# The sample state update as whole tiles on GpSimd, and a causal mask taken with a Relu, in an SSD mixer

## The chip, the core and the metric

The kernel runs on one core of one Trainium2 chip. The core has TensorE (PE, with its weight loads listed apart as PEld), VectorE (DVE), ScalarE (ACT), GpSimd (POOL) and SyncE (SP, which here only issues transfers). Each engine takes its instructions strictly in the order of its own queue and waits on semaphores for the others. The metric is the device time of one execution in microseconds (us).

## The reference, cut to what matters

One inference step of a trunk of two layers serves a prompt of 512 tokens and 8 samples of one token each. Layer 0 mixes tokens with sparse attention, layer 1 with a Mamba-2 state space mixer (SSD); each is followed by a squared-ReLU MLP. The change lies in the SSD mixer:

```python
a_cum = jnp.cumsum(chunk(dt * a), axis=2)
causal = np.tril(np.ones((L, L), dtype=bool))[:, :, None, None]
seg = a_cum[:, :, :, None] - a_cum[:, :, None, :]
decay = jnp.exp(jnp.where(causal, seg, NEG))
cb = jnp.einsum('bclgn,bcsgn->bclsg', cc, bc)
y_diag = jnp.einsum('bclsg,bclsgr,bcsgrp->bclgrp', cb, decay, xdt)
...
def step(state, inp):
    cs, cd = inp
    return state * cd[..., None, None] + cs, state
...
y_off = jnp.einsum('bclgn,bcgrpn,bclgr->bclgrp', cc, prev, jnp.exp(a_cum))
```

For the prompt there are 32 heads in 4 groups; a_cum is a cumulative sum of negative numbers along the tokens. For a sample the scan has one step: new state = old state * exp(dt a) + dt x B, and y = C . new state; the state of all samples is 8 x 32 x 64 x 128 numbers (8 MB), read from memory and written back.

## The kernel before, in words

Activations lie with the features on the 128 partitions and 520 columns (512 prompt tokens, 8 samples). Every large product is made of units of 24 or 48 matmuls with fp32r operands: weights are split into a high part (ScalarE copy, L330, tile `wh`) and a low part (VectorE subtraction, L336, tile `wh`), two products ahead of their use, and three terms are accumulated.

The mixer (`ssd`, L1643) walks a list `SSD_SEQ` over 16 pairs of heads, q = 0..15, four to a group. For each group `ssd_bc` makes B and C with a convolution each, B.C (`cb`, one 128x512 tile), the transposed B (`bt`) and the samples' B and C on all partitions (`bc`, 128 x 2 x 8 x 128). For each pair there are four steps:

- `x`: `ssd_x` makes the product and its convolution (`conv`, L1435: three VectorE multiply-adds of 128x512, a Tanh, one more VectorE operation, and small ones for the samples).
- `pair`: `ssd_pair` (L1503). Two matmuls spread a_cum of a head over the partitions, two more add the causal mask (`negsR`, 0 or -1e30); eight Exp on ScalarE with a bias give `M`, and VectorE multiplies it by `cb`. Another matmul (`sp`) and an Exp give `E` for the off-chunk term. Then come transposes of X, `xd`, the chunk states `st`, the outputs `yd` and `yo`, and `y`. At its end stands the sample update: for each of 8 samples ScalarE makes B times dt x (`xb`), VectorE the new state (L1462, tile `ss`) and, with a third operand and an accumulator, the sample's y. The state is loaded by SP (`ssd_state`) and stored by the GpSimd queue.
- `z`: `ssd_gate` makes the gate's product and multiplies y with it. The sum of squares `yss` is added up on GpSimd (L1602), one 128x520 addition for a pair.
- `out`: after the first pair of the next group, the output product of the group before (`ssd_out`, 8 units of 24 matmuls, added up by VectorE).

The `x` step of pair q+1 stands before the `pair` step of q in the list (after the next group's `bc` at the end of a group). The order in an engine's queue is not the order of the source alone: a scheduler, when the program is built, places instructions by their readiness in its own model of times, and by source order among the ready ones; so rows of neighbouring steps are interleaved. Tiles come from pools with a fixed number of buffers: `ss` 2, `xb` 3, `s` (PSUM) 4, `a` (PSUM, the large products) 2, `M` 2, `cv` 2, `z` 1.

Of the kernel before, what the change touches and what calls it, by code (L numbers as in the profile page):

```python
# [22 lines left out]
NEG = -1e30  # L23
# [3 lines left out]
CONST_COLS = [('ident', 128), ('tri', 128), ('e2', 32), ('negq', 128), ('negs', 128), ('selb', 256),  # L27
# [9 lines left out]
def shape_constants():  # L37
    c = np.zeros((128, NCONST), np.float32)

    def put(name, a):  # L40
        o, w = CONST_AT[name]
        c[:a.shape[0], o:o + w] = a

    i = np.arange(128)
    put('ident', np.eye(128, dtype=np.float32))
    put('negq', np.where(i[None, :] <= i[:, None], 0.0, NEG))
    put('tri', (i[:, None] <= i[None, :]).astype(np.float32))
    put('negs', np.where(i[:, None] <= i[None, :], 0.0, NEG))
    t = np.arange(4)[None, :, None] * 128 + i[:, None, None]
    ok = (16 * np.arange(32)[None, None, :] + 31 <= t) & (np.arange(32) < 31)  # L50
    put('cadd', np.where(ok, 0.0, NEG).reshape(128, 128))
    put('cmul', ok.astype(np.float32).reshape(128, 128))
    j, hc = i // 32, i % 32
    gp, r, e = hc // 8, (hc // 2) % 4, hc % 2
    live = hc < 16
    g = 2 * gp + e
    b = np.arange(8)
    put('selb', np.stack([(b[:, None] == 4 * k + j[None, :]) & live[None, :] for k in range(2)], 1)
        .astype(np.float32).reshape(8, 256))
    put('gsel', ((np.arange(16)[None, :] == (g * 4 + r)[:, None]) & live[:, None]).astype(np.float32))  # L60
    put('gmask', ((np.arange(4)[None, :] == g[:, None]) & live[:, None]).astype(np.float32))
    put('gsum', ((j[:, None] == j[None, :]) & (g[:, None] == g[None, :]) & live[:, None] & live[None, :]).astype(np.float32))
    put('sel2', (((j[:, None, None] == np.arange(4)[None, None, :]) & (r[:, None, None] == np.arange(4)[None, :, None])
                  & live[:, None, None]).astype(np.float32)).reshape(128, 16))
    put('e2', (i[:, None] % 32 == np.arange(32)[None, :]).astype(np.float32))
    put('jc', np.broadcast_to(np.arange(1, 7, dtype=np.float32), (128, 6)))
    return c
# [163 lines left out]
def ck(c):  # L231
    return slice(c * 128, (c + 1) * 128)
# [29 lines left out]
class Step:  # L262
# [393 lines left out]
    def setup_late(self):  # L656
# [6 lines left out]
        t = self.tile('s', [128, 256])  # L663
        self.aux(t[:, 0:128], I['const'][:, CONST_AT['negq'][0]:CONST_AT['negq'][0] + 128])
        self.aux(t[:, 128:256], I['const'][:, CONST_AT['negs'][0]:CONST_AT['negs'][0] + 128])
        self.negqR = self.const([128, 128], F32R, self.pn)
        self.vcopy(self.negqR, t[:, 0:128])
        self.negsR = self.const([128, 128], F32R)
        self.vcopy(self.negsR, t[:, 128:256])
# [687 lines left out]
    def dt_fin(self, ps):  # L1357
# [50 lines left out]
        self.nac, self.cd, self.dtde = (m[:, ck(n)].rearrange("p (c h) -> p c h", c=4) for n in range(3))  # L1408
        fl = "p c h -> p (c h)"
        self.ts(self.nac.rearrange(fl), p[:, 0:128], -1.0)  # L1410
# [53 lines left out]
    def ssd_bc(self, g, first):  # L1464
# [10 lines left out]
        self.copy(cb, p)  # L1475
# [27 lines left out]
    def ssd_pair(self, g, t, X, G, w):  # L1503

        q = 4 * g + t
        C, cb, bt, xs, bc = (G[k] for k in ('C', 'cb', 'bt', 'xs', 'bc'))
# [3 lines left out]
        for e in range(2):  # L1510
            r = slice(64 * e, 64 * e + 64)
            self.mm(ps[e], self.e2R[r, 2 * q + e:2 * q + e + 1].to_broadcast([64, 128]), self.ac2[r], True, False)
        for e in range(2):
            self.mm(ps[e].rearrange("p (c l) -> p c l", c=4), self.identR,
                    self.negsR[:, None, :].to_broadcast([128, 4, 128]), False, True)
        for e in range(2):
# [3 lines left out]
            for c in range(4):  # L1520
                self.act(m[:, ck(c)], p[:, ck(c)], AF.Exp, bias=self.nac[:, c, h:h + 1])
            self.tt(m, m, cb, ALU.mult)
            M.append(m)
        sp = self.tile('sp', [64, 2, 64], F32R)
        self.nc.gpsimd.tensor_copy(sp, self.e2R[0:64, 2 * q:2 * q + 2, None].to_broadcast([64, 2, 64]))
        p = self.tile('s', [128, 512])
        self.mm(p[:, 128:512], sp.rearrange("p a b -> p (a b)"), self.ac2[0:64, 128:512], True, True)
        E = self.tile('E', [128, 512])
        self.act(E[:, 128:512], p[:, 128:512], AF.Exp)
# [43 lines left out]

        x8 = self.small([128, 8], 'x8', 2)
        self.tt(x8, xs[:, 2 + t], self.sdb[:, q, 0, :], ALU.mult)
        ys = self.small([128, 8], 'ys', 2)
        for b in range(8):
            v = w[:, b]
            x = self.tile('xb', [128, 128])
            self.act(x, bc[0][:, b], AF.Copy, scale=x8[:, b:b + 1])  # L1580
            self.pool_stt(v, v, self.sdb[:, q, 1, b:b + 1], x, ALU.mult, ALU.add)
            self.stt(x, v, 1.0, bc[1][:, b], ALU.mult, ALU.mult, accum_out=ys[:, b:b + 1])
        self.store(self.O['ssm_s'][q], w.rearrange("p b n -> p (b n)"))
# [59 lines left out]
    def ssd(self, h):  # L1643
# [10 lines left out]
        X = {}  # L1654
        for kind, n in SSD_SEQ:
# [3 lines left out]
            elif kind == 'x':  # L1659
                G[g] = G_next  # L1660
                X[n] = self.ssd_x(g, t, G[g])
            elif kind == 'pair':
                y = self.ssd_pair(g, t, X.pop(n), G[g], self.ssd_state(n))
# [217 lines left out]
    def build(self, stop=None):  # L1881
# [17 lines left out]
        with self.tc.tile_pool(name='e', bufs=1) as self.pe:  # L1899
# [6 lines left out]
            with self.phase('s', {'g': 5, 'cv': 2, 'x': 2, 'th': 2, 'xd': 3, 'st': 2, 'M': 2, 'E': 1, 'y': 1, 'z': 1,  # L1906
                                  'acc': 8, 'bc': 1, 'ss': 2, 'xb': 3, 'yss': 1, 'yh': 8, 'sp': 1,
# [62 lines left out]
```

## Time and profile before

| what | value |
|---|---|
| median of the runs | 1722.26 us (3 runs, 1722.0 to 1723.0) |
| the profiled execution, its own time | 1719.56 us |
| its span in the trace | 1717.9 us |
| granted TensorE clock, mean | 0.993 of full speed |
| PE, PEld busy | 1664.7 us (97%), 1538.2 us (90%) |
| DVE, ACT, POOL busy | 984.0, 761.6, 143.5 us (57, 44, 8%) |

Busy time is the union of an engine's instructions. Matmuls are pipelined and their ends are modelled, so a busy PE can still lose time between two starts. A DVE or POOL row that waits for something after it has started counts that as its own duration. Starts are given in us from the span's beginning, and the mixer lies from about 888 to 1335.

### The profile page before, as it was taken

How to read it: one execution, taken by the hardware profiler on the slowest of the kernel's cores; microseconds unless marked ns; L12 is line 12 of the kernel's file. 1: busy time of each engine (PE TensorE's matmuls, PEld its weight loads, DVE VectorE, ACT ScalarE, POOL GpSimd, SP SyncE). 2: the span in 40 equal slices, each digit the busy share in tenths (PEclk: the TensorE clock that was granted, in tenths of full speed). 3: DMA queues.
4: the chain of work that ended last, by engine and by line, in shares of the span. 5: the costliest groups of instructions: out<-in, count | busy, mean ns of one | idle time of the engine just before them, and what ended most of it. 6: DMA issues, size and time to landing. Idle time of an engine off the chain costs nothing.

```text
span 1717.9 us, 34708 instructions
## 1 busy us (share of the span) xinstructions
PE 1664.7 (97%) x13878; PEld 1538.2 (90%) x13878; DVE 984.0 (57%) x2423; ACT 761.6 (44%) x1624; POOL 143.5 (8%) x303
## 2 busy tenths in 40 slices
PE   7899999999999999999999999999998999999997
PEld 6699877667989999999989898899987999999997
DVE  2543377776464343433478968879797643434344
ACT  3534366666443131322456666646564422323231
POOL 2000112310001000000001102111022000000000
PEclk9999999999999999999999999999999999999999
DMA  8822656545433523333433442344324232323321
GB/s 302 288 87 99 215 195 223 169 148 196 137 126 97 184 87 135 99 135 136 136 135 102 135 166 90 117 135 138 125 89 160 74 99 87 96 90 93 93 86 51
DMA packets 72114, 229.87 MB, mean 134 GB/s; under 512 B 8770, under 2 KB 15218, under 8 KB 71186
## 3 DMA queue, kind: packets, MB, share of 16 engines
q1 hardware_dynamic: 62546, 198.45, 35.1%
q0 software_dynamic: 8832, 28.16, 4.5%
q8 instruction: 109, 1.79, 0.4%
q10 hardware_dynamic: 576, 1.05, 0.2%
q14 instruction: 51, 0.42, 0.1%
HBM read 204.02 MB, written 23.61 MB: 133 GB/s over the span
## 4 chain that ended last, share of the span: by engine, by line
PE 71%; DVE 8%; ACT 2%; issue 1%; POOLq 0%; DMA 0%; SPq 0%; POOL 0%; DVEq 0%; ACTq 0%
PE a L323 60%; PE s L323 5%; PE f L323 2%; PE o L323 1%; DVE wh L336 1%; PE sc L323 1%; PE t L327 1%; DVE c L345 1%; DVE g L345 1%; ACT wh L330 1%; DVE acc L336 1%; PE s L327 0%; DVE ss L1462 0%; PE f L327 0%; ACT h L333 0%
## 5 line engine op out<-in xcount | busy, mean ns | idle before, releaser
L323 PE MATMUL a<-h,wh 128*128 128x256 f32 x5952 | 743.4, 284 | 3.8 <-ACT t L333 1.6
L323 PEld LDWEIGHTS a<-h,wh 128*128 128x128 f32 x5952 | 723.3, 189 | 10.1 <-issue 3.7
L330 ACT ACTIVATE wh<-w 128x1024 fp32r<-128x1024 f32 x212 | 224.5, 1059 | 521.8 <-PE a L323 480.4
L336 DVE TENSOR_TENSOR wh<-w,wh 128x1024 fp32r<-128x1024 f32 x212 | 259.6, 1225 | 266.4 <-ACT wh L330 265.8
L323 PEld LDWEIGHTS a<-hid,wh 128*128 128x128 f32 x3072 | 370.2, 188 | 5.0 <-issue 4.2
L323 PE MATMUL a<-hid,wh 128*128 128x256 f32 (+1 forms) x3072 | 373.7, 283 | 0.0
L336 DVE TENSOR_TENSOR t<-a,c 128x8 f32<-128x8 f32 x72 | 12.0, 167 | 217.4 <-PE a L323 217.4
L323 PE MATMUL a<-yh,wh 128*128 128x256 f32 (+1 forms) x768 | 98.4, 285 | 3.0 <-DVE acc L336 1.5
L323 PEld LDWEIGHTS a<-yh,wh 128*128 128x128 f32 x768 | 93.7, 188 | 5.2 <-DVE acc L336 2.2
L330 ACT ACTIVATE hid<-t 128x520 fp32r<-128x520 f32 x64 | 40.9, 639 | 84.5 <-DVE t L336 84.5
L330 ACT ACTIVATE h<-t 128x128 f32<-128x128 f32 (+3 forms) x128 | 52.5, 440 | 46.5 <-PE t L327 46.3
L333 ACT ACTIVATE h<-sc,m 128x128 f32<-128x128 f32 (+3 forms) x128 | 66.6, 530 | 14.6 <-DVE m L340 12.5
L336 DVE TENSOR_TENSOR hid<-t,hid 128x520 fp32r<-128x520 f32 x64 | 44.7, 700 | 42.3 <-ACT hid L330 42.3
L327 PE MATMUL t<-c,h 128*128 128x128 f32 x320 | 53.5, 281 | 1.9 <-DVE h L340 0.7
L345 DVE SCALAR_TENSOR_TENSOR c<-a,c,c 128x512 f32<-128x512 f32 (+1 forms) x74 | 53.9, 728 | 1.8 <-PE a L323 1.8
L333 ACT ACTIVATE xb<-bc,x 128x128 f32<-128x128 f32 x128 | 46.4, 419 | 15.8 <-DVE xb L345 11.2
L323 PE MATMUL sc<-kv,q 128*128 128x128 f32 (+3 forms) x128 | 49.5, 387 | 0.0
L323 PEld LDWEIGHTS a<-q,wh 128*128 128x128 f32 x384 | 46.3, 188 | 1.0 <-ACT wh L330 0.8
L327 PEld LDWEIGHTS t<-c,h 128*128 128x128 f32 x320 | 34.4, 141 | 13.8 <-issue 7.7
L323 PE MATMUL a<-q,wh 128*128 128x256 f32 (+1 forms) x384 | 46.7, 283 | 0.0
L323 PE MATMUL sc<-kv,c 128*128 128x128 f32 (+3 forms) x128 | 42.3, 331 | 4.2 <-POOL c L947 4.2
L1462 DVE SCALAR_TENSOR_TENSOR ss<-ss,c,xb 128x128 f32<-128x128 f32 x128 | 43.3, 361 | 4.4 <-ACT xb L333 4.2
(366 smaller groups left out, 1941.9 us busy)
## 6 DMA issues: line engine op xcount, KB each, us to landing
w<-in_w_dram SPq DMA_DIRECT2D x128, 512.0 KB, 3.5
w<-in_ada_w_dram SPq DMA_DIRECT2D x80, 512.0 KB, 3.6
w<-in_w_ssd_dram SPq DMA_DIRECT2D x40, 512.0 KB, 3.6
w<-in_w_nsa_dram SPq DMA_DIRECT2D x20, 512.0 KB, 3.6
ss<-in_ssm_dram SPq DMA_DIRECT2D x16, 512.0 KB, 4.3
out_ssm_s_dram<-ss POOLq DMA_DIRECT2D x16, 512.0 KB, 3.0
w<-in_w_sout_dram SPq DMA_DIRECT2D x16, 512.0 KB, 4.1
cm<-in_cmp_dram SPq DMA_DIRECT2D x24, 256.0 KB, 4.0
```

Source lines behind the costliest of these rows:

```text
L323: self.nc.tensor.matmul(out, lhsT, rhs, start=start, stop=stop, skip_group_check=True)
L327: self.nc.tensor.transpose(out, in_, self.C('ident')[0:k, 0:k])
L330: self.nc.scalar.activation(out, in_, AF.Copy, **kw)
L333: self.nc.scalar.activation(out, in_, f, **kw)
L336: self.nc.vector.tensor_tensor(out, a, b, op=op)
L345: self.nc.vector.scalar_tensor_tensor(out, a, s, b, op0=op0, op1=op1, **kw)
L1462: self.nc.vector.scalar_tensor_tensor(out, a, s, b, op0=op0, op1=op1)
```

## The change

The causal mask leaves the PSUM accumulation: `cb` is multiplied once a group by the 0/1 triangle `tri` (VectorE, in place of a ScalarE copy), the two mask matmuls of a pair go, and so that the exponential can't overflow above the diagonal, eight ScalarE Relu with scale -1 make max(0, a_s - a_l), over which two Exp of 128x512 with scale -1 are taken. `E` is read from the same two PSUM tiles (two Exp of 64x384), so that the `sp` copy on GpSimd and its matmul go. The constant `negs` and its loading go.

The sample update becomes a function of its own, called right after the `x` step, that is one pair earlier. It holds four GpSimd tensor-tensor operations over a whole 128 x 8 x 128 tile (state by its decay, B by dt x, their sum, the sum by C), and one VectorE reduction to the 8 numbers of y. The eight ScalarE and sixteen VectorE operations (with eight accumulator reads) of a pair go. `xb` becomes one buffer of 128 x 1024.

```diff
@@ ssd_bc
-        self.copy(cb, p)
+        self.tt(cb.rearrange("p (c l) -> p c l", c=4), p.rearrange("p (c l) -> p c l", c=4),
+                self.C('tri')[:, None, :].to_broadcast([128, 4, 128]), ALU.mult)
@@ ssd_pair
+    def ssd_sample(self, g, t, G):
         q = 4 * g + t
+        xs, bc = G['xs'], G['bc']
+        v = self.ssd_state(q)
+        x8 = self.small([128, 8], 'x8', 2)
+        self.tt(x8, xs[:, 2 + t], self.sdb[:, q, 0, :], ALU.mult)
+        sh = [128, 8, 128]
+        x = self.tile('xb', sh)
+        f = self.nc.gpsimd.tensor_tensor
+        f(v, v, self.sdb[:, q, 1, :, None].to_broadcast(sh), op=ALU.mult)
+        f(x, bc[0], x8[:, :, None].to_broadcast(sh), op=ALU.mult)
+        f(v, v, x, op=ALU.add)
+        f(x, v, bc[1], op=ALU.mult)
+        ys = self.small([128, 8], 'ys', 3)
+        self.nc.vector.tensor_reduce(ys, x, AX.X, ALU.add)
+        self.store(self.O['ssm_s'][q], v.rearrange("p b n -> p (b n)"))
+        return ys
...
-            self.mm(ps[e], self.e2R[r, 2 * q + e:2 * q + e + 1].to_broadcast([64, 128]), self.ac2[r], True, False)
-        for e in range(2):
-            self.mm(ps[e].rearrange("p (c l) -> p c l", c=4), self.identR,
-                    self.negsR[:, None, :].to_broadcast([128, 4, 128]), False, True)
+            self.mm(ps[e], self.e2R[r, 2 * q + e:2 * q + e + 1].to_broadcast([64, 128]), self.ac2[r], True, True)
...
-                self.act(m[:, ck(c)], p[:, ck(c)], AF.Exp, bias=self.nac[:, c, h:h + 1])
+                self.act(m[:, ck(c)], p[:, ck(c)], AF.Relu, scale=-1.0, bias=self.ac[:, c, h:h + 1])
+
+            self.act(m, m, AF.Exp, scale=-1.0)
             self.tt(m, m, cb, ALU.mult)
             M.append(m)
-        sp = self.tile('sp', [64, 2, 64], F32R)
-        self.nc.gpsimd.tensor_copy(sp, self.e2R[0:64, 2 * q:2 * q + 2, None].to_broadcast([64, 2, 64]))
-        p = self.tile('s', [128, 512])
-        self.mm(p[:, 128:512], sp.rearrange("p a b -> p (a b)"), self.ac2[0:64, 128:512], True, True)
         E = self.tile('E', [128, 512])
-        self.act(E[:, 128:512], p[:, 128:512], AF.Exp)
+        for e in range(2):
+            r = slice(64 * e, 64 * e + 64)
+            self.act(E[r, 128:512], ps[e][r, 128:512], AF.Exp)
...
-        x8 = self.small([128, 8], 'x8', 2)
-        self.tt(x8, xs[:, 2 + t], self.sdb[:, q, 0, :], ALU.mult)
-        ys = self.small([128, 8], 'ys', 2)
-        for b in range(8):
-            v = w[:, b]
-            x = self.tile('xb', [128, 128])
-            self.act(x, bc[0][:, b], AF.Copy, scale=x8[:, b:b + 1])
-            self.pool_stt(v, v, self.sdb[:, q, 1, b:b + 1], x, ALU.mult, ALU.add)
-            self.stt(x, v, 1.0, bc[1][:, b], ALU.mult, ALU.mult, accum_out=ys[:, b:b + 1])
-        self.store(self.O['ssm_s'][q], w.rearrange("p b n -> p (b n)"))
@@ ssd
                 X[n] = self.ssd_x(g, t, G[g])
+                Y[n] = self.ssd_sample(g, t, G[g])
             elif kind == 'pair':
-                y = self.ssd_pair(g, t, X.pop(n), G[g], self.ssd_state(n))
+                y = self.ssd_pair(g, t, X.pop(n), G[g], Y.pop(n))
```

## Rows read from the trace of the kernel before

**Rows 1.** The page: busy us, share of the span, instructions of PE.

```profile
PE 1664.7 (97%) x13878; PEld 1538.2 (90%) x13878; DVE 984.0 (57%) x2423; ACT 761.6 (44%) x1624; POOL 143.5 (8%) x303
```

**Rows 2.** Busy time by stretch: the four stretches that are dense with pairs.

```profile
core 0: us, PE busy (x) PEld busy (x) DVE busy (x) ACT busy (x) POOL busy (x), PEclk, DMA share, GB/s
913.40:1000.70 87.30, 86.78 (x688) 79.06 (x688) 79.94 (x238) 62.48 (x171) 14.36 (x28) 1.00 0.42 142
1038.60:1104.20 65.60, 64.73 (x517) 58.87 (x515) 57.76 (x161) 42.92 (x115) 11.90 (x21) 1.00 0.35 116
1143.40:1209.20 65.80, 65.09 (x531) 60.27 (x529) 59.22 (x164) 42.77 (x107) 11.99 (x22) 1.00 0.37 116
1248.60:1292.00 43.40, 43.15 (x350) 37.78 (x351) 40.04 (x118) 27.09 (x74) 8.77 (x12) 1.00 0.29 88
```

**Rows 3.** The same stretches, tile xb alone: us, DVE busy, ACT busy.

```profile
913.40:1000.70 87.30, 17.11 (x96) 11.24 (x32) 1.00 0.42 142
1038.60:1104.20 65.60, 11.31 (x57) 6.96 (x19) 1.00 0.35 116
1143.40:1209.20 65.80, 12.52 (x57) 6.78 (x19) 1.00 0.37 116
1248.60:1292.00 43.40, 10.98 (x48) 5.94 (x16) 1.00 0.29 88
```

**Rows 4.** PE in time order: start us, us, then line and operation; one pair's start.

```profile
1157.76 1.16 PE L323 MATMUL s<-c,c 64*128 64x512 f32 x4
1158.85 0.43 PE L323 MATMUL s<-c,sp 64*128 64x384 f32 x1
1159.22 0.66 PE L327 MATMUL s<-c,x 128*128 128x128 f32 x4
```

**Rows 5.** DVE groups by form, 1143.4 to 1209.2: busy us, mean ns, idle before.

```profile
L336 DVE TENSOR_TENSOR wh<-w,wh 128x1024 fp32r<-128x1024 f32 x9 | 11.0, 1222 | 3.1 <-ACT wh L330 3.1
...
L345 DVE SCALAR_TENSOR_TENSOR st<-st,c,s 128x64 f32<-128x64 f32 x18 | 4.0, 274 | 0.0
...
L345 DVE SCALAR_TENSOR_TENSOR y<-x,c,s 128x512 f32<-128x512 f32 x3 | 2.2, 742 | 0.0
...
L1462 DVE SCALAR_TENSOR_TENSOR x<-th,x 128x512 f32<-128x512 f32 x3 | 2.1, 693 | 0.7 <-ACT th L333 0.7
...
L336 DVE TENSOR_TENSOR xd<-s,c 128x512 f32<-128x512 f32 x3 | 2.0, 676 | 0.0
```

**Rows 6.** POOL and ACT by tile: duration ns min/median/max, first and last start.

```profile
L1602 POOL TENSOR_TENSOR yss<-yss,z x14: 1289/1311/1572, 950.5 to 1279.8; 128x520 f32<-128x520 f32 x14
...
L1525 POOL CAST sp<-c x16: 281/333/898, 888.5 to 1264.5; 64x128 fp32r<-64x128 f32 x16
...
L333 ACT ACTIVATE M<-s,c x128: 352/380/423, 915.1 to 1277.5; 128x128 f32<-128x128 f32 x128
```

**Rows 7.** POOL's memset of three columns, a group: busy us, mean ns, idle.

```profile
L1439 POOL MEMSET cv<- 128x3 f32 x24 | 2.4, 102 | 77.7 <-DVE xs L340 33.1 <-DVE xs L1454 12.6 <-DVE x L345 12.6
```

**Rows 8.** DVE and POOL in time order around two additions of L1602.

```profile
949.43 0.74 DVE L345 SCALAR_TENSOR_TENSOR x<-cv,c,x 128x512 f32<-128x512 f32 x1
950.47 1.57 POOL L1602 TENSOR_TENSOR yss<-yss,z 128x520 f32<-128x520 f32 x1 [1.54 <-ACT z L333]
950.79 1.80 DVE L345 SCALAR_TENSOR_TENSOR x<-cv,c,x 128x512 f32<-128x512 f32 x1
...
1174.27 0.68 DVE L336 TENSOR_TENSOR xd<-s,c 128x512 f32<-128x512 f32 x1
1174.64 1.30 POOL L1602 TENSOR_TENSOR yss<-yss,z 128x520 f32<-128x520 f32 x1 [3.02 <-ACT z L333]
```

**Rows 9.** Waits of PE, and of SP's queue, in the mixer: us, times, longest.

```profile
PE s L323 <- DVE xd L336: 1.2, 5, 0.3
...
SPq L351 <- DMA out_ssm_s_dram<-ss: 45.5, 12, 11.7
```

**Rows 10.** A table load on ACT within the mixer.

```profile
891.72 1.28 ACT L333 ACT_TABLE_LOAD   x1
```

More of the change, by code (lines that the diff above doesn't have):

```diff
@@ L23 @@
 NEG = -1e30
-CONST_COLS = [('ident', 128), ('tri', 128), ('e2', 32), ('negq', 128), ('negs', 128), ('selb', 256),
+CONST_COLS = [('ident', 128), ('tri', 128), ('e2', 32), ('negq', 128), ('selb', 256),
               ('cadd', 128), ('cmul', 128), ('gsum', 128), ('gsel', 16), ('gmask', 4), ('sel2', 16), ('jc', 6)]
@@ L47, in shape_constants @@
     put('tri', (i[:, None] <= i[None, :]).astype(np.float32))
-    put('negs', np.where(i[:, None] <= i[None, :], 0.0, NEG))
     t = np.arange(4)[None, :, None] * 128 + i[:, None, None]
@@ L662, in setup_late @@
         self.tt(self.wg[1], wg, self.wg[0], ALU.subtract)
-        t = self.tile('s', [128, 256])
+        t = self.tile('s', [128, 128])
         self.aux(t[:, 0:128], I['const'][:, CONST_AT['negq'][0]:CONST_AT['negq'][0] + 128])
-        self.aux(t[:, 128:256], I['const'][:, CONST_AT['negs'][0]:CONST_AT['negs'][0] + 128])
         self.negqR = self.const([128, 128], F32R, self.pn)
         self.vcopy(self.negqR, t[:, 0:128])
-        self.negsR = self.const([128, 128], F32R)
-        self.vcopy(self.negsR, t[:, 128:256])
         u = self.U('np')
@@ L1407, in dt_fin @@
         m = self.m[0].rearrange("p a b -> p (a b)")
-        self.nac, self.cd, self.dtde = (m[:, ck(n)].rearrange("p (c h) -> p c h", c=4) for n in range(3))
+        self.ac, self.cd, self.dtde = (m[:, ck(n)].rearrange("p (c h) -> p c h", c=4) for n in range(3))
         fl = "p c h -> p (c h)"
-        self.ts(self.nac.rearrange(fl), p[:, 0:128], -1.0)
+        self.vcopy(self.ac.rearrange(fl), p[:, 0:128])
         self.copy(ae, p[:, 128:256])
@@ L1501, in ssd_state, with ssd_pair @@
         return w
-    def ssd_pair(self, g, t, X, G, w):
+    def ssd_sample(self, g, t, G):
         q = 4 * g + t
-        C, cb, bt, xs, bc = (G[k] for k in ('C', 'cb', 'bt', 'xs', 'bc'))
+        xs, bc = G['xs'], G['bc']
[13 more added lines that the diff above has]
+        return ys
+    def ssd_pair(self, g, t, X, G, ys):
+        q = 4 * g + t
+        C, cb, bt, xs = (G[k] for k in ('C', 'cb', 'bt', 'xs'))
         M = []
@@ L1653, in ssd @@
         first = [pb]
-        X = {}
+        X, Y = {}, {}
         for kind, n in SSD_SEQ:
@@ L1906, in build @@
             with self.phase('s', {'g': 5, 'cv': 2, 'x': 2, 'th': 2, 'xd': 3, 'st': 2, 'M': 2, 'E': 1, 'y': 1, 'z': 1,
-                                  'acc': 8, 'bc': 1, 'ss': 2, 'xb': 3, 'yss': 1, 'yh': 8, 'sp': 1,
+                                  'acc': 8, 'bc': 1, 'ss': 2, 'xb': 1, 'yss': 1, 'yh': 8,
                                   'sq': 'M', 'x7': 'M', 'ssq': 'st', 'ad': 'xd', 'dt': 'acc'}) as self.ps, \
```

## The prediction, made before the change was run

> **What bounds the kernel now.** I read the engine shares first: TensorE is busy for 97% of the span [rows 1], so outside the mixer nothing that the change touches can matter. Within the mixer I cut the time at the stretches that are dense with pairs, between them lie the output products. There PE is busy 98 to 99%, but DVE is not far behind: 79.94 of 87.30 us, 57.76 of 65.60, 59.22 of 65.80 and 40.04 of 43.40, some 90% [rows 2]. ACT has a third of its time free and POOL most of it. PE waits for DVE hardly ever, 1.2 us in five places for `xd` [rows 9], so today PE sets the pace and DVE keeps up with little to spare. The change takes work from both and gives POOL much; whether DVE still keeps up is what decides.
>
> **PE.** In one pair's start the four matmuls of `ps` take 1.09 us from the first start to the start of the next group, of which the two mask matmuls are half, 0.545; the `sp` matmul takes 0.37 to the transposes' start [rows 4]. A pair saves 0.915 us, sixteen pairs 14.6 us. This is the most that the change can bring while PE sets the pace.
>
> **ACT.** The `xb` work (6.78 of 42.77 us in the third stretch [rows 2, 3]) goes. Eight Relu stand where eight Exp stood, at the same 0.38 us [rows 6]. Two Exp of 128x512 and one more `E` Exp are new. No row shows an Exp of that size; it costs between one and four of the 128x128 rows, 0.38 to 1.52 us, so three new ones cost at most 4.6 us a pair, 14 us in a stretch with three pairs: 42.77 - 6.78 + 14 = 50 of 65.8 us, still free. I count ACT at nothing; its cover is that spare time. That a Relu between the Exp makes ACT load a table is not seen in a row: the bounds are nothing and two loads of 1.28 us a pair [rows 10], and even these fit into the spare time. I take nothing.
>
> **DVE's own work.** The whole `xb` work goes: 17.11, 11.31, 12.52 and 10.98 us of the four stretches [rows 3]. Added is one reduction of 128x1024 for each `x` step (`ssd_sample` follows it). The nearest row is the subtraction over as many columns, 1.22 us [rows 5], of which some 0.08 overlap with the next; I take 1.14, with bounds of 1.0 and 1.3. There are three `x` steps in the third stretch [rows 5]; by the code's list I count 4, 3, 3 and 2. The masked `cb` adds 0.6 in each of the first three (an operation of 128x512 is 0.68 to 0.74 us with its overlap [rows 5]). What is left as DVE's own is 79.94 - 17.11 + 4.56 + 0.6 = 68.0 us, and in the same way 50.5, 50.7 and 31.3.
>
> **POOL's four operations.** The only row of this kind has 520 columns: 1.311 us at the median [rows 6]. In proportion 1024 columns are 2.58; with the 0.10 of a memset of three columns [rows 7] as the fixed part they are 0.10 + 1.21 x 1024/520 = 2.48. From below: POOL's copy with one input takes 0.28 us at best for 128 columns [rows 6], (0.28 - 0.10)/128 = 1.4 ns a column, 1.54 us for 1024, if an operand that repeats one number costs no read. I take 2.48, as all four have two inputs like the row, and keep 1.54 to 2.6 for the range.
>
> [...]
>
> **What POOL does to DVE.** This is the term that turns the sign. While POOL adds `yss`, a DVE operation with two SBUF operands doesn't run: the convolution's multiply-add takes 0.74 us alone and 1.80 us when it starts into the addition, and ends 0.55 us after it; the addition itself, begun at 950.47 beside a running DVE operation, takes 1.57 instead of 1.31 [rows 8]. So each waits for the other, for a whole instruction. An operation with one operand in PSUM is not held: `xd` from 1174.27 and an addition from 1174.64 overlap, and both take their usual 0.68 and 1.30 us [rows 8].
>
> [...]
>
> So in a dense stretch DVE's time is its own work, plus POOL's operations, less what DVE does beside them without the lock. Whether it idles at the reduction or is held by the lock makes no difference. I count POOL's operations: four for each `x` step, of which one in a stretch falls outside, as the decay of the state needs no `x8` and can run early, or as the last comes late: 15, 11, 11 and 8 (the fourth has its two whole), 37.2, 27.3, 27.3 and 19.8 us. What runs beside them: in the third stretch `st`, `y` and `xd`, which read PSUM, make 4.0 + 2.2 + 2.0 = 8.2 us [rows 5], and the reductions 3.4; of these 11.6 I take 8 as covered, and in proportion to the own work 11, 8, 8 and 5 (bounds: none, and all of it with as much again of the kinds that I left out, 16). DVE's time is then
>
> 68.0 + 37.2 - 11 = 94.2 against 87.3: +6.9
> 50.5 + 27.3 - 8 = 69.8 against 65.6: +4.2
> 50.7 + 27.3 - 8 = 70.0 against 65.8: +4.2
> 31.3 + 19.8 - 5 = 46.1 against 43.4: +2.7
>
> Together +18.0 us. This lets DVE idle nowhere else, though in these four stretches it idled 25 us before (262.1 - 236.96 [rows 2]); of that I leave an eighth, +3. Between the stretches, where DVE has few rows, PE keeps its gain for three pairs: -2.7. The sum is +18.3, rounded +19 for the first pair's burst, which I did not count.
>
> **What moves with it.** The state's load is issued on SP one pair earlier, and its store on POOL's queue after the four operations. SP waits 45.5 us in all for such stores today, and PE for none of it [rows 9]; with two `ss` buffers and a burst that ends a pair before its `y` I count nothing. Behind a burst of four (10 us, some 13 with DVE's turns between) stand on POOL the memset and copy of the next convolution, `ssm_p`'s store and `yss`, whose tile `z` has one buffer. The `x` steps follow each other at 22 us on the mean (three in 65.8 us [rows 2, 5]), so this costs nothing while POOL starts at once; a late start is part of rival (c). The reduction waits for POOL at the head of DVE's queue, and behind it stand the next pair's `M` and `xd`, for which PE waits. The setup's one load and copy less lie off the path: nothing.
>
> **The rivals.**
> (a) *PE goes on setting the pace.* If POOL's operations take p us, the four sums give 45 p - 93.6 + 0.3 = 45 p - 93.3 with the 3 us and the -2.7; the sign turns at p = 2.07. At the lower bound of 1.54, or at 2.48 with twice the cover (64 us instead of 32), the sum is at -14 or below, DVE keeps up everywhere in the dense stretches, and the gain is PE's 14.6 us at most: 1708. For it: PE absorbs the 1.3 us holds of today. Against: the row of 1.311 for half the columns. Chance 0.23.
> (b) *A wash*: p near 2.07 to 2.15, or the lead of two products in the weights hides more of DVE's lag: 1719 to 1726. Chance 0.13.
> (c) *The reduction blocks DVE.* If the queue's order, made when the program is built, puts the reduction before POOL can be done, DVE idles through the bursts and the 32 us of cover are lost: +19 + 32, some 1773. For it: a model that ignores the lock. Against: the order of before left PE almost no wait. Chance 0.10.
> The forecast, slower by the lock, has 0.54.
>
> **How the numbers follow.** The sum is made on the profiled execution (1719.56 us, span 1717.9); the median of the runs is 1722.26, 2.7 above, and a difference carries over. 1722.3 + 19 = 1741.3. The forecast's own range is 1727 (p = 2.2) to 1760 (half of the cover lost). For eight in ten I go from 1711, which leaves out the fullest gain of (a), to 1766, which leaves out most of (c). A measurement of this kernel tells some 0.2% (3.4 us) from no change. Faster takes (a) and a little of (b), 0.25; same 0.12; slower takes the forecast and (c), 0.63.
>
> **What the profile afterwards would show.** Right: POOL rows of 128x1024 at 2.4 to 2.6 us, 64 of them; DVE rows with two SBUF operands of 2 us and more beside them; DVE busy in the dense stretches near 100% although its own work has shrunk; PE idle before `xd`, `M` and `wh` rows in the tens of us. The `ps` group of a pair at 0.55 us either way. Wrong: POOL operations under 2 us, or holds that are short, and the mixer shorter by some 14 us. A long idle of DVE before the reduction would show (c).

## The result and the profile after

The changed kernel takes 1787.20 us at the median of its runs (1781.31 to 1791.49), the kernel before 1722.55 beside it: 3.7% slower, ratio 1.0372 with a 95% interval of [1.0351, 1.0393]. The forecast said slower by 19 us; it is 65 by the medians. The profiled execution took 1786.26 us, with a span of 1784.6.

The page of the changed kernel, its busy times (us, share of the span, instructions) and its chain of waits by engine (followed back from the last instruction to what released each step), and below them the chain of the kernel before:

```profile
PE 1690.4 (95%) x13830; PEld 1554.9 (87%) x13830; DVE 973.4 (55%) x2058; ACT 747.8 (42%) x1540; POOL 281.8 (16%) x350
...
PE 60%; DVE 11%; POOL 6%; ACT 2%; issue 2%; DMA 1%; POOLq 0%; SPq 0%; DVEq 0%; ACTq 0%
...
PE 71%; DVE 8%; ACT 2%; issue 1%; POOLq 0%; DMA 0%; SPq 0%; POOL 0%; DVEq 0%; ACTq 0%
```

Against [rows 1] POOL's busy time has doubled and DVE's has shrunk by 11 us. On the chain PE has fallen from 71% to 60%, DVE has risen from 8% to 11%, and POOL, with nothing before, holds 6%.

**Where the 67 us of span lie.** I cut both traces at two POOL instructions that the change doesn't touch: the `acc` memset (L1371, now L1367) with which the mixer begins, and the first `st` addition (L534, now L533) after the last pair. From that addition to the end both kernels take the same, 412.8 us. Between the two marks, "the mixer" from here on, the kernel before takes 416.85 us and the changed one 474.06: +57.2. The other 9.4 lie ahead of the mixer, in attention, which the change leaves alone. There the granted clock of one stretch differs. Stretches of the changed kernel: in its first profile, and below in a second profile of the same code (columns: stretch, us, busy time of each engine with its instructions, granted clock, DMA share, GB/s):

```profile
220.00:240.00 20.00, 20.00 (x111) 13.57 (x111) 6.45 (x25) 9.47 (x27) 0.58 (x2) 0.50 0.03 2
```

```profile
220.00:240.00 20.00, 19.96 (x197) 14.81 (x196) 13.60 (x54) 15.40 (x46) 2.96 (x7) 1.00 0.35 114
```

In the first, PE works through this stretch without a pause at a granted clock of 0.50 and runs 111 matmuls; in the second it stays at 1.00 and runs 197. In the 20 us ahead of it PE was busy for 17.4 us in the first and 16.2 in the second, with a mean granted clock of 0.83 in both; what decides between the two isn't shown here. Four more runs of the changed kernel fell in two groups, 1779.4 and 1780.1 against 1788.4 and 1791.8 us. Profiles of experiments show the low stretch with the old samples' update and with the new one, with the setup edit and without it. So 9 to 10 of the 67 us come or stay away with the single execution, and the change itself costs the 57 us of the mixer. The second profile gives 474.06 us for the mixer again.

**Inside the mixer.** Waits between the two marks of the changed kernel (us in all, times, longest):

```profile
DVE ys L1515 <- POOL xb L1513: 51.8, 16, 6.0
POOL ss L1510 <- DMA ss<-in_ssm_dram: 32.0, 9, 7.9
PE s L322 <- DVE xd L335: 22.4, 10, 7.8
POOL xb L1511 <- DVE x L335: 13.4, 10, 2.9
PE a L322 <- DVE c L347: 10.6, 2, 5.3
PE a L322 <- DVE acc L335: 5.1, 2, 3.1
PE s L322 <- ACT xd L329: 4.2, 3, 2.4
```

The reduction waits for POOL in all sixteen pairs, 51.8 us, and PE's wait for `xd` has gone from 1.2 us [rows 9] to 22.4. POOL waits for DVE's `x8` (dt x, printed as `x<-xs,c`) in turn. One pair shows how the pieces hang together. DVE, PE and POOL of the changed kernel in order of time (start us, us, instruction, idle before it):

```profile
1076.27 0.17 DVE L335 TENSOR_TENSOR x<-xs,c 128x8 f32<-128x8 f32 x1
...
1083.40 1.22 DVE L1515 TENSOR_REDUCE ys<-xb 128x8 f32<-128x1024 f32 x1 [3.84 <-POOL xb L1513]
...
1090.78 1.75 DVE L344 SCALAR_TENSOR_TENSOR y<-xs,c,ys 128x8 f32<-128x8 f32 x1
...
1095.38 0.68 DVE L335 TENSOR_TENSOR M<-M,g 128x512 f32<-128x512 f32 x1
...
1096.83 0.17 DVE L335 TENSOR_TENSOR x<-xs,c 128x8 f32<-128x8 f32 x1
```

```profile
1076.52 1.90 POOL L1511 TENSOR_TENSOR xb<-bc,x 128x1024 f32<-128x1024 f32 x1 [1.90 <-DVE x L335]
1078.50 2.39 POOL L1512 TENSOR_TENSOR ss<-ss,xb 128x1024 f32<-128x1024 f32 x1
1080.97 2.40 POOL L1513 TENSOR_TENSOR xb<-ss,bc 128x1024 f32<-128x1024 f32 x1
...
1090.15 2.35 POOL L1510 TENSOR_TENSOR ss<-ss,c 128x1024 f32<-128x1024 f32 x1
```

```profile
1089.70 1.16 PE L322 MATMUL s<-xd,g 128*128 128x128 f32 x8 [1.04 <-DVE xd L335]
1090.61 4.30 PE L322 MATMUL a<-h,wh 128*128 128x256 f32 x34
1096.99 0.73 PE L322 MATMUL s<-M,xd 128*64 128x128 f32 x4 [2.08 <-DVE x L335]
```

`x8` ends at 1076.44, and three POOL operations follow one after the other, B times x (1.90 us), the sum and the product with C (2.39 and 2.40), to 1083.37. DVE has less than that to do between `x8` and the reduction, so it stands idle for 3.84 us; `xd` comes late and PE waits 1.04 us. In ten of the sixteen pairs B times x begins within 0.1 us of the end of `x8`, and in all sixteen the reduction starts 6.8 to 8.6 us after B times x: this chain of three, with the reduction close behind `x8` in DVE's queue, is the wait. Then POOL's next operation begins at 1090.15, and `y<-xs,c,ys`, eight columns, 0.22 us otherwise, takes 1.75 and ends when POOL does. DVE doesn't idle from there to 1097.00, so all that stands behind it in its queue moves back, `M` at 1095.38 and the next `x8` at 1096.83, which the view names as what PE waited for, and PE idles 2.08 us. What follows is one more cost. The same place of the changed kernel in stretches of 5 us (the last three columns: granted clock, DMA share, GB/s):

```profile
1095.00:1100.00 5.00, 3.00 (x15) 1.76 (x15) 3.20 (x12) 4.57 (x14) 2.94 (x3) 0.74 0.02 3
1100.00:1105.00 5.00, 5.00 (x21) 3.63 (x19) 1.88 (x2) 1.14 (x4) 4.82 (x4) 0.50 0.02 8
1105.00:1110.00 5.00, 5.00 (x31) 4.33 (x30) 4.42 (x9) 3.70 (x9) 0.00 (x0) 0.73 0.65 215
1110.00:1115.00 5.00, 5.00 (x49) 4.50 (x47) 4.96 (x7) 3.98 (x14) 4.22 (x3) 1.00 0.36 107
```

From the idle time on the granted clock is 0.74, 0.50 and 0.73 in three stretches: (0.26 + 0.50 + 0.27) x 5 = 5.2 us of full-speed work lost at this place, more than the idle time itself (1.04 + 2.08). Summed in this way over stretches of 5 us, the changed kernel loses 18.8 us of its mixer to the lower clock, the kernel before nothing. (Some 2.4 of the 18.8 fall into idle time: weighted with PE's busy share in stretches of 1 us they are 16.4.) The 57.2 us are then +43.4 of PE's idle time (4.4 before, 474.06 - 426.30 = 47.8 after), +18.8 of lower clock, and -5.0 of PE's work at full speed, which is what is left over. Not every stop costs clock: in the 5 us from 1162.7 PE is busy for 1.9, and the granted clock stays at 1.00 there and in the 5 us behind.

### The profile page after: what moved, and what is told of

Read it like the earlier page. It is cut to its first block, busy times and chain, and to the rows that moved or that the text cites. A ratio compares the mean times of both kernels' runs of the same rounds, so it can differ in the third digit from the quotient of the medians.

```text
span 1784.6 us, 34130 instructions
## 1 busy us (share of the span) xinstructions
PE 1690.4 (95%) x13830; PEld 1554.9 (87%) x13830; DVE 973.4 (55%) x2058; ACT 747.8 (42%) x1540; POOL 281.8 (16%) x350
## 3 DMA queue, kind: packets, MB, share of 16 engines
q10 hardware_dynamic: 576, 1.05, 0.2%
## 4 chain that ended last, share of the span: by engine, by line
PE 60%; DVE 11%; POOL 6%; ACT 2%; issue 2%; DMA 1%; POOLq 0%; SPq 0%; DVEq 0%; ACTq 0%
PE a L322 52%; PE s L322 2%; POOL ss L1512 2%; POOL xb L1513 2%; DVE wh L335 2%; PE f L322 2%; POOL xb L1511 1%; PE o L322 1%; PE sc L322 1%; DVE x L344 1%; PE t L326 1%; DVE c L344 1%; DVE yh L344 1%; DVE M L335 1%; DVE acc L335 1%
## 5 line engine op out<-in xcount | busy, mean ns | idle before, releaser
L322 PE MATMUL a<-h,wh 128*128 128x256 f32 x5952 | 757.3, 286 | 3.7 <-ACT t L332 1.6
L335 DVE TENSOR_TENSOR wh<-w,wh 128x1024 fp32r<-128x1024 f32 x212 | 267.7, 1263 | 268.7 <-ACT wh L329 266.6
L322 PE MATMUL a<-yh,wh 128*128 128x256 f32 (+1 forms) x768 | 106.3, 295 | 16.8 <-DVE c L347 10.6
L322 PEld LDWEIGHTS a<-yh,wh 128*128 128x128 f32 x768 | 98.7, 196 | 22.4 <-DVE c L347 11.1
L332 ACT ACTIVATE h<-sc,m 128x128 f32<-128x128 f32 (+3 forms) x128 | 66.5, 530 | 14.6 <-DVE m L339 12.5
L1367 POOL MEMSET acc<- 128x160 f32 x1 | 0.2, 237 | 347.6 <-DVE h L335 347.6
L1515 DVE TENSOR_REDUCE ys<-xb 128x8 f32<-128x1024 f32 x16 | 19.5, 1220 | 51.8 <-POOL xb L1513 51.8
L965 DVE TENSOR_REDUCE m<-sc 128x1 f32<-128x384 f32 (+1 forms) x64 | 38.0, 616 | 17.0 <-PE sc L322 16.9
```

The costliest lines, as they stand in the source:

```text
L322: self.nc.tensor.matmul(out, lhsT, rhs, start=start, stop=stop, skip_group_check=True)
L332: self.nc.scalar.activation(out, in_, f, **kw)
L335: self.nc.vector.tensor_tensor(out, a, b, op=op)
L965: self.nc.vector.tensor_reduce(m[:, k:k + 1], ss[k][:, 0:w], AX.X, ALU.max)
L1367: nc.gpsimd.memset(x, 0.0)
L1515: self.nc.vector.tensor_reduce(ys, x, AX.X, ALU.add)
```

## The experiments

All figures of the mixer are between the two marks; PE's idle time is the mixer less PE's busy time there; "clock" is the sum over 5-us stretches of their length times one less the granted clock. "POOL" is the busy time of the whole-tile operations on it, "wait" DVE's at the reduction. The ratios below are against runs of the kernel before beside each experiment, whose medians were 1721.3 to 1729.3 us; the mixer's time doesn't hold the low stretch in attention and is the better measure.

| kernel | mixer us | PE idle | clock | DVE busy | POOL | wait |
|---|---|---|---|---|---|---|
| before | 416.9 | 4.4 | 0.0 | 348.7 | - | - |
| changed | 474.1 | 47.8 | 18.8 | 338.7 | 147.0 | 51.8 |
| mask half alone | 415.2 | 9.6 | 1.7 | 349.8 | - | - |
| samples' half alone | 488.6 | 56.9 | 25.6 | 359.0 | 147.7 | 38.6 |
| reduction without the wait | 446.4 | 31.5 | 8.5 | 356.3 | 146.6 | - |
| no GpSimd operations | 416.3 | 9.4 | 3.4 | 308.0 | - | - |
| reduction at the pair's end | 469.6 | 42.9 | 18.8 | 355.4 | 150.6 | 24.5 |
| eight memsets | 418.9 | 11.2 | 1.7 | 316.5 | 122.9 | 2.7 |
| ten memsets | 426.5 | 14.2 | 8.5 | 321.0 | 153.3 | 4.8 |
| two of four operations | 429.8 | 17.1 | 8.6 | 330.8 | 62.5 | - |
| mask half, B x on GpSimd | 435.4 | 25.7 | 8.6 | 357.5 | 38.3 | - |
| mask half, no copies | 419.9 | 9.7 | 1.7 | 350.5 | - | - |
| mask half, whole tiles on DVE | 433.5 | 20.2 | 13.7 | 375.6 | - | - |

### The two halves

The mask half is the diff ahead of the prediction without `ssd_sample`; the pair keeps the eight steps at its end.

```
-                Y[n] = self.ssd_sample(g, t, G[g])
-                y = self.ssd_pair(g, t, X.pop(n), G[g], Y.pop(n))
+                y = self.ssd_pair(g, t, X.pop(n), G[g], self.ssd_state(n))
```

> The change's mask half alone: B.C masked once a group, Relu then Exp in M, E straight from the spread matmuls, one constant less in the setup; the samples' update stays in eight steps at the pair's end. The prediction's own first term says TensorE gets 0.915 us a pair less, 14.6 us in all: 1708 us if nothing else moves. If the stretch of lower clock between 217 and 242 us of the changed kernel comes with the setup edit (mixer starts 9.4 us late), it shows here too and the time is near 1717. If TensorE was not what bounded the pairs, 1722 (the kernel before). If the Relu costs table loads, above 1740.

Measured: 1719.71 us, ratio 0.9988 [0.9958, 1.0018]: no difference, so the 14.6 us of the first theory don't come, and the case of TensorE not bounding the pairs fits. The mixer doesn't start late (887.68 us): the setup edit costs nothing.

The samples' half keeps the mask matmuls, `negs`, `sp` and the eight Exp, and takes `ssd_sample` as changed.

> The change's other half alone: the samples' update as four whole-tile GpSimd operations one pair ahead, the mask left as in the kernel before (matmuls with the negative triangle, setup as before). [...] Theory B, that the two halves hurt together (ScalarE's Relu in the way, or the setup's low clock): the time is below 1765. The prediction's lock sum alone, without its saving of 14.6: 1756.

Measured: 1798.62 us, ratio 1.0413 [1.0353, 1.0473]. The whole loss is the samples' half. The kernel before with the mixer's 57 us and all of the 14.6 on top would be 1722 + 57 + 14.6 = 1794, and the run is 4.6 us above that; its profile has the low clock ahead of the mixer too (mixer start 897.09), without the setup edit. Beside GpSimd's work the mask half is worth 488.6 - 474.1 = 14.6 us of mixer. That this is the sum of the prediction's first step is chance: 9.1 of it are less idle time of PE and 6.8 less low clock, and none is less work of PE. Alone it is worth 1.6.

### The wait and the holds, taken apart

```
-        self.nc.vector.tensor_reduce(ys, x, AX.X, ALU.add)
+        self.nc.vector.tensor_reduce(ys, bc[1], AX.X, ALU.add)
```

> The changed kernel, but the reduction reads the group's C tile in place of GpSimd's product, so VectorE has no wait for GpSimd; the samples' part of y is left out, all GpSimd operations stay. Theory A1, the wait of the reduction at the head of VectorE's queue is the loss: the 51.8 us of VectorE's wait go, and with them most of the mixer's 57 us: 1725 to 1740. Theory A2, the prediction's lock (VectorE held while GpSimd works, whatever it waits for): the loss stays within 10 us, 1776 to 1787.

The second kernel has this edit too, and the four operations are out, so the new state isn't made.

> The changed kernel without the four GpSimd operations; the reduction reads the group's C tile, the states are stored as loaded, so the samples' update and their y are left out. This is the floor: neither wait nor lock. Theory A1 and A2 both expect the mixer at or under that of before (460 us) less TensorE's 14.6: 1700 to 1712, with 9 more if the low clock before the mixer stays. [...]

Measured: 1750.13 us without the wait (1.0137 [1.0079, 1.0195]), 1728.06 without GpSimd's operations (1.0001 [0.9974, 1.0029]). The first lies between its two ranges; the second misses its 1700 to 1712, because the mixer without GpSimd's operations, 416.3 us, is as long as that of before (416.9, not the 460 of the expectation): neither PE's 14.6 us nor DVE's saved work shortens it. Rows between the two marks, first without the wait, then without the operations:

```profile
889.24:1335.68 446.44, 414.91 (x3323) 382.51 (x3321) 356.31 (x629) 241.71 (x565) 199.44 (x161) 0.98 0.36 119
```

```profile
890.65:1306.99 416.34, 406.94 (x3323) 378.57 (x3321) 307.96 (x629) 240.97 (x565) 53.79 (x98) 0.99 0.38 128
```

The same 629 DVE instructions take 308.0 us alone and 356.3 beside GpSimd: 48.4 us of holds for 146.6 us of GpSimd's operations, a third of them. The operations, with what hangs on them, cost the mixer 30.1 us. The wait for the product costs another 27.6 (474.06 - 446.44). So the two theories share the loss; A1, by which most of it would have gone, and A2, by which all of it would have stayed, both miss. In the changed kernel itself the holds are 30.7 us (338.7 - 308.0), since DVE idles through a part of GpSimd's time. How a hold looks, in the kernel without the wait:

```profile
1026.95 2.77 POOL L1513 TENSOR_TENSOR xb<-ss,bc 128x1024 f32<-128x1024 f32 x1
1027.39 2.74 DVE L335 TENSOR_TENSOR y<-y,E 128x384 f32<-128x384 f32 x1
...
1251.85 2.76 POOL L1513 TENSOR_TENSOR xb<-ss,bc 128x1024 f32<-128x1024 f32 x1
1252.29 0.68 DVE L335 TENSOR_TENSOR acc<-acc,a 128x520 f32<-128x520 f32 x1
1252.89 1.21 DVE L1515 TENSOR_REDUCE ys<-bc 128x8 f32<-128x1024 f32 x1
```

An addition with two SBUF operands (0.55 us alone) takes 2.74 and ends 0.41 us after GpSimd's; one with an operand in PSUM (`a`) and the reduction take their usual 0.68 and 1.21. No row before the change had a reduction beside GpSimd; in this kernel all sixteen took 1.20 to 1.22 us, beside its operations or not.

The other edit moves the wait instead of removing it: the four operations begin after the pair before (for the first pair of a group still after its `x` step), and the reduction stands at the end of its own pair.

```
+                if t < 3:
+                    Y[n + 1] = self.ssd_sample(g, t + 1, G[g], S)
...
+        self.nc.vector.tensor_reduce(ys, xy, AX.X, ALU.add)
         self.stt(y[:, 512:T], xs[:, 2 + t], self.dsk[:, q:q + 1], ys, ALU.mult, ALU.add)
```

> The changed kernel, complete, with the four GpSimd operations of a pair begun after the pair before it and the reduction moved from the head of VectorE's queue to the end of its own pair, so VectorE should find the product ready. [...] Theory A2 (one loss that only changes its place: the wait turns up again at the pair's end): 1775 to 1790.

Measured: 1774.11 us, 1.0314 [1.0285, 1.0343], 0.9 us below A2's range and 24.0 above the run without the wait (1750.13), to which it would come if only the holds were left. Waits of this kernel in the mixer:

```profile
PE s L322 <- DVE xd L335: 29.5, 9, 5.0
DVE ys L1584 <- POOL xb L1512: 24.5, 7, 6.0
...
PE s L322 <- DVE M L335: 6.7, 3, 3.6
```

The wait has halved, and the holds have grown by 16.7 us of DVE's busy time (355.4 against 338.7). My reading, which no run tests by itself, is that an engine that idles less at the reduction meets GpSimd's operations more often. The mixer is 4.5 us shorter, PE waits as long for DVE as before. Where the product isn't needed at all, 27.6 us come back; where it is only needed later, 4.5 do.

### Is it GpSimd's length, or what it reads?

GpSimd gets eight or ten memsets of the same two tiles in place of the four operations; the reduction goes on waiting for the last.

```
-        f = self.nc.gpsimd.tensor_tensor
-        f(v, v, self.sdb[:, q, 1, :, None].to_broadcast(sh), op=ALU.mult)
...
+        f = self.nc.gpsimd.memset
+        f(v, 0.0)
...
```

> The changed kernel with GpSimd's four tensor operations a pair replaced by eight memsets of 128x1024, of about the same time, which read nothing of SBUF; the samples' update is left out, the reduction still waits for GpSimd. Theory A1 with the lock as the holds' cause: VectorE's operations are no longer held, its busy time in the mixer falls from 339 us by about 30 to near 308, and the wait stays: mixer 444 us, 1750 to 1762. If memsets hold VectorE as the tensor operations do: 1775 to 1790.

> As the run with memsets, but ten of them a pair, 9.6 us, a little longer than the four tensor operations of the changed kernel (9.2 us by their mean); the samples' update is left out. If the wait of the reduction needs only GpSimd's length, it comes back to near 52 us, and the mixer rises from 419 to about 445. If both wait and loss come from the shared access of GpSimd's and VectorE's tensor operations, the wait stays under 12 us and the mixer at 418 to 425.

Measured: eight memsets (0.96 us each, 7.7 a pair) 1733.33 us, 1.0070 [1.0042, 1.0097]; ten (9.6 us a pair, against 9.2 for the four operations) 1733.40, 1.0021 [0.9980, 1.0063]. Both reach what the kernel without GpSimd operations reaches within 2.6 and 10.2 us of mixer, and I had expected the first at 1750 or more; the second comes within 1.5 us of the 418 to 425 us of mixer that were expected with a short wait. The waits of the one with ten:

```profile
PE s L322 <- ACT xd L329: 6.4, 3, 5.3
...
DVE ys L1521 <- POOL xb L1519: 4.8, 2, 4.6
...
PE s L322 <- DVE xd L335: 2.8, 4, 1.0
```

With GpSimd busy for longer than in the changed kernel the wait at the reduction is 4.8 us instead of 51.8, and PE's for `xd` 2.8 instead of 22.4. For the wait this proves less than I had expected of it, for the edit takes away more than the reads: a memset has no operand, so it waits neither for `x8` nor for B. GpSimd runs ahead of the pairs, and the reductions moved with it. In the kernel with ten, the last memset, the last reduction and the last `x8` in order of time:

```profile
1198.61 0.95 POOL L1519 MEMSET xb<- 128x1024 f32 x1
1215.59 1.22 DVE L1521 TENSOR_REDUCE ys<-xb 128x8 f32<-128x1024 f32 x1
1280.20 0.17 DVE L335 TENSOR_TENSOR x<-xs,c 128x8 f32<-128x8 f32 x1
```

The last reduction stands 65 us ahead of the last `x8`; in the changed kernel it starts 6.9 us after it. So the chain of three operations behind `x8`, which makes the wait there, is cut here, and whether operations of this length in that chain would wait without reading anything stays untested.

For the holds the runs say more. Beside the memsets the additions and nearly all of the products that the operations had held ran at their usual times: four of the sixteen additions `y<-y,E`, which took up to 2.74 us beside the operations, ran beside one of the ten memsets, all at 0.55 or 0.56 us; of the products `M<-M,g` sixteen did, fourteen of them at their usual 0.68 or 0.69, one at 1.05, and one at 5.82 behind an instruction of another kind (last section). 13.0 us of DVE's busy time stay over the 308.0 without GpSimd, against 48.4, and most of them lie in that other kind. One reservation: a memset is also shorter than an operation (0.96 us against 1.9 to 2.6), and this experiment doesn't tell length and reads apart.

### Half a dose

```
-        f(v, v, x, op=ALU.add)
-        f(x, v, bc[1], op=ALU.mult)
```

> The changed kernel with only two of the four GpSimd operations (decay times state, B times x), and the reduction over the group's C tile, so nothing waits for GpSimd: half a dose of the holds (the samples' sum is left out). If the holds cost in proportion to GpSimd's time (30 us of mixer for 146 us of GpSimd operations): 63 us of them cost 13: mixer 429 us, 1730 to 1738. If VectorE's slack swallows the first half: 1718 to 1726.

Measured: 1732.23 us, 1.0066 [1.0022, 1.0110]; its profile has the low clock ahead of the mixer. The mixer grows by 13.5 us over that without operations, as the first theory puts it: 62.5 us of operations add 22.9 us of holds (330.8 - 308.0) and 13.5 of mixer, 146.6 us add 48.4 and 30.1. There is no first part that DVE's spare time swallows whole: it is 0.6 us of mixer for each us of hold in both.

### Where the mask half's saving goes

> The mask half alone, without the eight scaled copies a pair on ScalarE (45 us in the mixer); VectorE's state update reads B directly, so the samples' product with x is left out, and all else is as in the mask half's run. Theory M1: the Relus' and the second Exp's time on ScalarE (27 us more in the mixer) is what eats TensorE's saving; with ScalarE relieved the mixer falls from 415.2 us by 8 to 12: 403 to 407, 1706 to 1712. Theory M2: VectorE or TensorE's order of work eats it, not ScalarE: 413 to 417, 1716 to 1721 (12 more in an execution with the low clock before the mixer).

The edit drops the `AF.Copy` line and gives `bc[0][:, b]` to the state's step. Measured: 1729.08 us, 1.0008 [0.9976, 1.0039], mixer 419.9. ScalarE lost 37.5 us of its work (279.0 to 241.5) and nothing was gained, so M1 falls; the mixer is 2.9 us above M2's range. In the mask half's run PE's work at full speed is 403.9 us (415.2 - 9.6 - 1.7), 8.5 less than the 412.4 of before, not 14.6. The tile `s` alone, then `a` alone, of the mask half's run between the marks (columns as above, without POOL in the second):

```profile
887.68:1302.89 415.21, 100.07 (x761) 70.25 (x761) 57.34 (x159) 88.40 (x316) 0.00 (x0) 1.00 0.39 129
```

```profile
887.68:1302.89 415.21, 340.54 (x2551) 315.42 (x2550) 28.07 (x59) 29.04 (x49) 1.00 0.39 129
```

`s` has lost 10.9 us against the kernel before (110.97 for 809 matmuls), but `a` takes 340.5 where it took 331.8 for 2562. The product matmuls between the pairs' own are spread longer. What holds them by a few ns each isn't in any wait of the trace, and I leave it open.

### Two candidates

The first keeps the mask half and gives GpSimd only the product of B and x, after the pair before; the second keeps it and does the whole-tile operations on VectorE at the pair's end.

> A candidate: the mask half, and of the samples' update only the product B times x on GpSimd as one whole-tile operation after the pair before (1.89 us a pair), which takes eight scaled copies a pair off ScalarE; VectorE's sixteen operations stay as before. If ScalarE is what eats the mask half's saving (the chain's share of ScalarE rose from 2% to 4% in that run): 1719 less up to 8, plus 6 for holds in proportion: 1711 to 1719. If GpSimd's holds weigh more than the copies: 1722 to 1735.

> A candidate: the mask half, and the samples' update as the change's whole-tile operations but on VectorE at the pair's end, none on GpSimd and no copies on ScalarE. VectorE pays four operations of about 1.14 to 1.22 us and the reduction of 1.22, 5.8 to 6.1 us a pair, against 5.7 in the kernel before (361 + 314 + 81 ns eight times); ScalarE is relieved of 46 us. Theory M1 (ScalarE eats the mask half's saving): 1708 to 1714. Theory M2: 1718 to 1726. If whole-tile operations of over 1 us each delay VectorE's short ones on TensorE's path: 1726 to 1740.

Measured: 1742.65 us, 1.0147 [1.0105, 1.0189], and 1747.24 us, 1.0097 [1.0051, 1.0144], both above all that was expected. The one operation a pair took 2.40 us instead of 1.89, and 38.3 us of it cost 20.2 us of mixer over the mask half's. Two things are seen: DVE's first step of the state waits for the product, 9.0 us in five waits, and `y<-xs,c,ys` takes 809 ns on the mean in place of 223, 9.3 us in all. The second has none of the update on GpSimd, and still PE waits for DVE's `acc`, `c` and `z` (8.8, 4.6 and 3.3 us, the longest 4.6). Two causes stand side by side and weren't parted: the update is more work for DVE, 98 us against 72 in the mask half's run (DVE busy 375.6 against 349.8; the sum of single rows in the expectation left out that they overlap), and five operations of 1.2 us and more stand in DVE's queue where PE's PSUM tiles have to be emptied. No version here beats the kernel before; the mask half alone equals it.

### The changed kernel again

> The changed kernel itself once more, on another chip, to see how much of its 67 us is the stretch of low clock before the mixer (217 to 242 us of its first profile). Theory C1: that stretch is an event of single executions of any kernel of this case (profiles of experiments with the same code before the mixer have it or not), so the mixer's growth of 57 us to its update's first sum (474 us against 417) returns within 5 us, and times fall in two groups: 1776 to 1782 without the event, 1786 to 1794 with it. Theory C2: the change brings the event itself: every execution lies above 1784 and its profile has a granted clock near 0.50 between 220 and 240 us.

Measured: 1784.24 us, 1.0375 [1.0321, 1.0429], in the two groups named above; the mixer took 474.06 us as in the first profile, with 47.8 us of idle time. C1 holds.

## Why the prediction was right in sign and wrong in size

**PE's saving, 14.6 us: too large.** Alone it is 1.6 us of mixer. The pair's own matmuls got cheaper by 10.9 us of 14.6; the products in between took most of it back. The step took a difference of starts within one pair [rows 4] for a difference in the mixer's time, though a PE that is 98% busy can still have slack between its matmuls; in the mask half's run the products took 8.8 us more for nearly as many matmuls.

**ACT at nothing: right.** The new Exp rows took 0.646 us (128x512) and 0.488 (64x384), 1.73 us a pair more, below the bound of 4.6. There are two table loads in the mixer, as many as before. Taking 37.5 us from ACT changed nothing.

**DVE's own work: right.** 36.5 us less in the four stretches by the sum; 40.7 less in the mixer (348.7 to 308.0 without GpSimd's operations). The reduction took 1.22 us.

**POOL's price of 2.48 us: a little high.** The four operations took 2.14, 1.98, 2.62 and 2.46 us by their means in the changed kernel, 2.30 over the 64, with holds in them; undisturbed rows are 1.90 where an operand repeats one number and 2.35 to 2.40 with two full ones. The groups by form:

```profile
L1512 POOL TENSOR_TENSOR ss<-ss,xb 128x1024 f32<-128x1024 f32 x16 | 41.9, 2617 | 1.2
L1513 POOL TENSOR_TENSOR xb<-ss,bc 128x1024 f32<-128x1024 f32 x16 | 39.3, 2458 | 0.9
L1510 POOL TENSOR_TENSOR ss<-ss,c 128x1024 f32<-128x1024 f32 x16 | 34.2, 2136 | 33.6 <-DMA ss<-in_ssm_dram 32.0 <-ACT c L329 1.5
L1511 POOL TENSOR_TENSOR xb<-bc,x 128x1024 f32<-128x1024 f32 x16 | 31.6, 1978 | 21.7 <-DVE x L335 13.4 <-DMA bc<-dr 7.5 <-DVE ys L1515 0.8
```

The undisturbed rows with two full operands lie 0.08 to 0.13 us below 2.48; the mean mixes the two kinds. But a lower price would have made the forecast worse: by 45 p - 93.3 the measured mean of 2.30 gives +10. So it isn't a term of the sum that was mis-sized; the sum is of the wrong kind.

**POOL's holds as a balance of DVE's time: the step that failed.** What the prediction calls the lock is the mutual wait of [rows 8]. The prediction set DVE's saved work and its spare time off against what GpSimd takes from it, and read the mixer's growth from what was left over. The loss itself was not far off: DVE is held for 30.7 us in the changed kernel and idles for 51.8 at the reduction, 82.5 us for all 64 operations, where the sum had 111.6 - 32 = 80 for the 45 that it counted. No row before showed the 3.4 us of reductions in that cover running beside POOL's operations; in the changed kernel every reduction waited for POOL's last operation instead, and in the kernel without the wait they took 1.20 to 1.22 us, whether POOL worked or not. What failed is the setting off. DVE's 40.7 us less of own work buy nothing: without GpSimd's operations the mixer is 0.5 us shorter than before. Nor does the spare time cover the loss: own work, holds and idle time make 308.0 + 82.5 = 390.5 us, less than the 416.9 of the mixer before, and yet the mixer grew by 57.2. DVE is busy 71% of it (338.7 of 474.1), and 42.7 of 55 us around the place shown, not "near 100%", which stood there as the sign of being right. In the rows shown it counts which instruction is late and who waits behind it: an idle of 3.84 us or a hold of 1.5 on a late `y` delays `xd` or `M`, and PE stands still. The half dose shows the same from the first us on (0.6 us of mixer for a us of hold).

**"Whether it idles at the reduction or is held by the lock makes no difference": wrong.** With the same operations on GpSimd, DVE loses 48.4 us to them where the reduction doesn't wait and 82.5 where it does, and the mixer is 27.6 us shorter in the first case. The mechanism of rival (c) was there in all sixteen pairs: the reduction stood in the queue where POOL could not be done. (c) put +32 on the forecast's +19 and came to +51, 1773; the mixer measured +57.2, some 1779 us in executions without the low attention stretch. I gave it 0.10 because before the change PE hardly waited, but that order had nothing to wait for on GpSimd, so it was no evidence. That its sum has nearly the right size is luck: it lost 32 us of cover on top of a balance that gave 19, where the runs show 27.6 for the wait and 30.1 for GpSimd's operations without it.

**PE's clock: a term that was missing.** Some 16 to 19 of the 57.2 us are lower clock after PE's idle times, and none of the steps had it. The kernel before shows the granted clock at 1.00 throughout its mixer, with 4.4 us of PE's idle time in all.

**What moves with it.** SP's waits for the state's stores have grown from 45.5 us [rows 9] to 113.9, and POOL waits 32.0 us for the state's load, which I had counted at nothing; what of it reaches PE wasn't tried by itself. The setup edit at nothing is right: the mask half's mixer began at 887.68 us, that of the kernel before at 888.30.

**The chances.** Slower had 0.63 and came. The sign was right by a mechanism that was there in part, the size was not. The range ended at 1766 because (c) was left out of it. Two bounds were added up wrongly: p = 2.2 gives 1728, not 1727, and half of the cover lost 1757, not 1760; neither matters here.

## What to carry to other kernels

Work moved to GpSimd doesn't simply free VectorE: here VectorE was held for 48.4 us by 146.6 us of GpSimd's operations, a third of their time, most of it in instructions with two SBUF operands (`y<-y,E` took 1.48 us on the mean, and 0.55 without them). Price the move by these holds, and don't pay them with VectorE's saved work or spare time; follow each hold to the instruction behind it that TensorE needs. An instruction that waits for another engine at the head of an in-order queue is priced by the chain that it waits for (here three operations behind an operand that VectorE itself delivers late), together with what is queued behind it; in this kernel the two costs added up (27.6 us of mixer for the wait, 30.1 for the operations). Where TensorE runs almost without a pause, making it wait can cost clock as well: here 18.8 us of clock came with 43.4 of idle time, though the smaller stops of the kernel before, 4.4 us in all, cost none.

## What the hardware showed that was not expected

- An operand that repeats a number along its last axis made GpSimd's 128x1024 operation cheaper: in the kernel without the wait the state's decay and the product with x take 2.10 and 1.95 us by their means, those with two full operands 2.56 and 2.55. Undisturbed it is 1.90 against 2.35 to 2.40, so not as cheap as the lower bound of 1.54 had it.
- Beside GpSimd's memsets it is VectorE's TENSOR_SCALAR that took longer: in the kernel with ten of them `xs<-xs,c`, eight columns, takes 841 ns on the mean of 24 (20.2 us), in the one without GpSimd operations 226 (5.4 us). Once it took 5.96 us, to the end of a row of memsets back to back, and the next two rows with it. The rows of that place:

```profile
1046.04 5.96 DVE L339 TENSOR_SCALAR xs<-xs,c 128x8 f32<-128x8 f32 x1
1046.17 5.82 DVE L335 TENSOR_TENSOR M<-M,g 128x512 f32<-128x512 f32 x1
1046.82 5.18 DVE L1458 SCALAR_TENSOR_TENSOR x<-th,x 128x512 f32<-128x512 f32 x1
```

- A whole attention stretch of 20 us ran at a granted clock of 0.50 in one execution and of 1.00 in another of the same kernel; that alone moved this kernel's time by 9 to 10 us (0.5%), so that a change of 0.2% can't be told from single runs.
